# Two decoder layers on one Trainium2 core: the forget-gate strips with the weights as the stationary operand

## Chip, core and metric

The kernel runs on one core of a Trainium2 chip. The metric is device time in microseconds (us) of one execution, the median of several runs. The engines are named as in the profile: PE (TensorE: matmuls), PEld (TensorE's loads of the stationary operand), DVE (VectorE), ACT (ScalarE), POOL (GpSimd), SP (the queue that issues most transfers).

## Reference

Each of two layers computes, for 256 positions of width 2048, a mixer (sliding-window attention beside a gated linear recurrence, HGRN2), a SwiGLU feed-forward part and a gated per-layer embedding. The change touches the forget gate of the recurrence, `hf`, which is 1024 of the 5632 columns of the input projection:

```python
proj = h @ w_in                       # h = rms_norm(x, gain): (256, 2048) @ (2048, 5632)
q, k, v, hq, hf, hi, hg = jnp.split(proj, SPLIT_POINTS, axis=-1)
...
z = hf.astype(jnp.float32)
f = lbf + (1.0 - lbf) * jax.nn.sigmoid(z)
log_f = jnp.log(f)
k_in = (1.0 - lbf) * jax.nn.sigmoid(-z)
hq_ = jax.nn.silu(hq.astype(jnp.float32))
...
o = hgrn2_chunkwise(hq_, k_in, hi, log_f)   # per head of 128 features
```

`rms_norm` divides each position by its own root mean square. The kernel multiplies the gain into the transposed input and applies the factor 1/rms of a position, `rx`, only to the finished product.

## The kernel before

All large products run in "strips" of 512 output columns. A strip takes its weights in chunks of 256 rows. For each chunk `load_w` issues one transfer of 512 KB on SP (tile `wr`), ACT rounds it to an fp32r tile `wh` (line 173) and DVE makes the remainder `wl` (line 174); `wh` and `wl` have 8 buffers each, so that the rounding may run one strip of 8 chunks ahead. The transposed input is kept in the same way as a high and a low part (`xh`, `xl`, both in tiles `ck`), and a product is the sum of three matmuls: xh by wh (line 231), xl by wh (232) and xh by wl (234). In `strip` the input is the stationary operand (128 features by the 128 positions of one half `t`) and the weights are the moving one, 512 columns. The accumulators `acc` then have positions on the partitions and features along the row. One strip of the input projection is 16 row tiles x 2 halves x 3 = 96 matmuls.

After each chunk `tick()` lets other work in: generators that were handed to `start` (attention, recurrence) take one step, and functions that were handed to `later(n, ...)` run n ticks on. That and a scheduler set where the small matmuls stand between those of a strip. Each engine then works through its own list in order.

The strips of the input projection come in this order: keys and values, two strips of attention queries (`done_q(half)`), and then, for each of two groups of four recurrence heads, forget gate, recurrence query, recurrence input, output gate. The recurrence needs its forget gate with features on the partitions. `done_f` (lines 594 to 611) therefore copies the accumulator with the factor `rx` (a scalar for each partition, line 596), and two ticks later `turn` transposes the four blocks on PE (line 601), takes two sigmoids on ACT (603, 604) into `s.f` and `s.k`, and applies the lower bound on DVE (607, 609). This happens for each half `t`, so twice in a strip and 8 times in the program.

The attention on the first query strip runs beside the second one. In it PE computes scores (line 515), DVE takes row maxima, ACT the exponentials (534, 538), DVE the sums (539) and their reciprocals (540). For the second half of the positions, ACT copies scores out of PSUM (526) before DVE masks them (527). Small matmul results stand in four PSUM banks, `ms`, which `bank()` hands out in turn.

Of the kernel before, what the change touches and what calls it, by code (L numbers as in the profile page):

```python
# [8 lines left out]
F32 = mybir.dt.float32  # L9
F32R = mybir.dt.float32r  # L10
I32 = mybir.dt.int32
AF = mybir.ActivationFunctionType
ALU = mybir.AluOpType
AX = mybir.AxisListType

P = 128
SEQ = 256
NT = 2
# [6 lines left out]
W = 512  # L25
# [21 lines left out]
def decoder(ctx: ExitStack, tc: tile.TileContext, x, p, positions, w_in, attn_sinks,  # L47
# [11 lines left out]
    sm = ctx.enter_context(tc.tile_pool(name="sm", bufs=2))  # L59
    pacc = ctx.enter_context(tc.tile_pool(name="pacc", bufs=4, space=PSUM))  # L60
    pms = ctx.enter_context(tc.tile_pool(name="pms", bufs=4, space=PSUM))

    V, S, G, T = nc.vector, nc.scalar, nc.gpsimd, nc.tensor
# [7 lines left out]
    def later(n, fn):  # L71

        queue.append((clock[0] + n, fn))
# [3 lines left out]
    @contextmanager  # L77
    def behind(*names):

        with ExitStack() as st:  # L80
            for n in names:
                st.enter_context(tc.issue_after(marks[n].ins))
            yield
# [3 lines left out]
    def start(gen):  # L87

        running.append(gen)
        if next(gen, True):  # L90
            running.remove(gen)

    def tick():
        clock[0] += 1
        for gen in list(running):
            if next(gen, True):
                running.remove(gen)
        for item in [q for q in queue if q[0] <= clock[0]]:
            queue.remove(item)
            item[1]()  # L100

    def nat(shape=(P, W), dt=F32):
        return np_.tile(list(shape), dt, tag="nat", name="nat")

    def bank(shape=(P, W)):
        return pms.tile(list(shape), F32, tag="ms", name="ms")
# [5 lines left out]
    ident = cp.tile([P, P], F32, name="ident")  # L112
# [11 lines left out]
    ps = bank()  # L124
    T.transpose(ps[:, 0:32], g0rows, ident[0:32, 0:32])
    S.preload_act_table(AF.Copy)
    first = V.tensor_copy(gT[:, 0:32], ps[:, 0:32])
# [39 lines left out]
    def square_sum(src, acc, shape=(P, W)):  # L167
        j = np_.tile([P, W], F32, tag="junk", name="junk", bufs=1)
        S.activation(j[:, 0:shape[1]], src, AF.Square, accum_out=acc)  # L169

    def split(src, hi, lo):

        a = S.copy(hi, src)  # L173
        v = V.tensor_tensor(lo, src, hi.bitcast(F32), op=ALU.subtract)  # L174
        return a, v
# [27 lines left out]
    def new_ck():  # L203
        return [xp.tile([P, 4, SEQ], F32R, tag="ck", name="ck", bufs=14) for i in range(2)]
# [4 lines left out]
    def load_w(w, c, col):  # L209

        raw = wpr.tile([P, 2, W], F32, tag="wr", name="wr")
        nc.sync.dma_start(raw, w[c * 2 * P:(c + 1) * 2 * P, col:col + W].rearrange(
            "(k p) n -> p k n", p=P))
        hi = wps.tile([P, 2, W], F32R, tag="wh", name="wh")
        lo = wps.tile([P, 2, W], F32R, tag="wl", name="wl")
        marks["hi"], marks["lo"] = split(raw, hi, lo)
        return hi, lo

    def strip(lhs, w, col, done, nch=8, row0=0, skew=0, psum=None, pre=None):

        ps = psum or [pacc.tile([P, W], F32, tag="acc", name=f"acc{t}") for t in range(NT)]
        ws = {}

        def part(t, c, lows=(0, 1)):
            hi, lo = ws[c]
            for k in range(2):
                kt = 2 * c + k
                xh, xl = (a[:, kt % 4, t * P:(t + 1) * P] for a in lhs[kt // 4])
                first, last = kt == 0, kt == 2 * nch - 1
                if 0 in lows:  # L230
                    T.matmul(ps[t], xh, hi[:, k], start=first, stop=False)  # L231
                    T.matmul(ps[t], xl, hi[:, k], start=False, stop=False)  # L232
                if 1 in lows:
                    marks[t, c] = T.matmul(ps[t], xh, lo[:, k], start=False, stop=last)  # L234

        for i in range(nch + skew):
            if pre:
                pre(i)
            if i < nch:
                with behind("x") if pre and i == 0 else nullcontext():  # L240
                    ws[i] = load_w(w, row0 // (2 * P) + i, col)
                if pre and i == 0:
                    for t in range(NT):
                        part(t, i, (0,))
                    for t in range(NT):
                        part(t, i, (1,))
                    tick()
                    continue
                part(0, i)
                if i == nch - 1:  # L250
                    done(0, ps[0])
            if i >= skew:
                part(1, i - skew)
            tick()
        done(1, ps[1])

    def load_gain(g, col):
        b = np_.tile([P, W], F32, tag="gB", name="gB", bufs=2)
        nc.sync.dma_start(b, g[col:col + W].partition_broadcast(P))
        return b  # L260
# [22 lines left out]
    def lazy_rstd(ss, name):  # L283
        got = {}

        def get(t):
            if t not in got:
                got[t] = sum_rstd(ss[t], D, f"{name}{t}")
            return got[t]
        return get  # L290


    ones = cp.tile([P, P], F32, name="ones")
# [6 lines left out]
    lb = cp.tile([P, DEPTH, 8], F32, name="lb")  # L300
    omlb = cp.tile([P, DEPTH, 8], F32, name="omlb")
# [101 lines left out]
    xT = [new_ck() for c in range(4)]  # L403
# [21 lines left out]
    for l in range(DEPTH):  # L425

        rx = lazy_rstd(ss, "rx")
        wi = w_in[l]
# [9 lines left out]
        def tables(t):  # L438
            if t not in rot:
                r = rx(t)  # L440
                tb = sm.tile([P, 4, 32], F32, name=f"rot{t}", bufs=1)
                for i, (a, f) in enumerate(((cos, 0.125), (sin, 0.125), (cos, 1.0), (sin, 1.0))):
                    V.tensor_scalar(tb[:, i], a[:, t], r[:, 0:1], f, op0=ALU.mult, op1=ALU.mult)
                rot[t] = tb
            return rot[t]
# [29 lines left out]
        def done_q(half):  # L475
            qT[half] = sp.tile([P, 4, SEQ], F32, tag="AB"[half], name="qT")

            def done(t, ps):
                tb = tables(t)
                o = nat()  # L480
                ov = o.rearrange("p (j g two d) -> p g j two d", j=4, g=2, two=2)
                rotate(ps, tb, 0, 8, ov[:, :, :, 0], ov[:, :, :, 1])
                start(attend(half, t, o))
            return done
# [97 lines left out]
        class Rec:  # L582
# [8 lines left out]
                s.at = sp.tile([P, NT, 4, P], F32, tag="at", name="at")  # L591
                s.ax = sp.tile([P, 4, P], F32, tag="ax", name="ax")

            def done_f(s, t, ps):
                z = nat()
                S.activation(z, ps, AF.Copy, scale=rx(t)[:, 0:1])

                def turn():
                    pt = bank((P, 4, P))
                    for b in range(4):  # L600
                        T.transpose(pt[:, b], z[:, b * P:(b + 1) * P], ident)
                    cols = slice(t * P, (t + 1) * P)
                    S.activation(s.f[:, :, cols], pt, AF.Sigmoid)
                    S.activation(s.k[:, :, cols], pt, AF.Sigmoid, scale=-1.0)
                    for h in range(4):
                        c = s.grp * 4 + h
                        V.tensor_scalar(s.f[:, h, cols], s.f[:, h, cols], omlb[:, l, c:c + 1],
                                        lb[:, l, c:c + 1], op0=ALU.mult, op1=ALU.add)
                        V.tensor_scalar(s.k[:, h, cols], s.k[:, h, cols], omlb[:, l, c:c + 1],
                                        None, op0=ALU.mult)  # L610
                later(2, turn)

            def done_q(s, t, ps):
                sg = nat()
# [176 lines left out]
        if l == 0:  # L791
            with tc.issue_after(first.ins):
                strip(xT, wi, 1024, done_kv, pre=load_x)
        else:
            strip(xT, wi, 1024, done_kv, skew=4)
        for half in range(2):
            strip(xT, wi, half * W, done_q(half))
        for grp in range(2):
            rec = Rec(grp)
            strip(xT, wi, 2560 + grp * W, rec.done_f)  # L800
            strip(xT, wi, 1536 + grp * W, rec.done_q)
            strip(xT, wi, 3584 + grp * W, rec.done_i)
            strip(xT, wi, 4608 + grp * W, rec.done_g)
# [5 lines left out]
        xT = [new_ck() for c in range(4)]  # L809
        mg = []  # L810
        for s in range(4):
            gB = load_gain(post_mix_gain[l], s * W)

            def done(t, ps, s=s, gB=gB):
                if t == 0:
                    mg.append(sp.tile([P, NT, W], F32, tag="ABCD"[s], name=f"mg{s}"))
                V.tensor_tensor(mg[s][:, t], ps, gB, op=ALU.mult)
                square_sum(ps, ssm[t][:, s:s + 1])
                if s == 3:
                    post_norm(mg, ssm, t, ss, xT, gain_cols(32, l, 16), 4)  # L820
# [8 lines left out]
        for gi, glen in enumerate(FF_GROUPS):  # L829
            hid = []  # L830
            for j in range(glen):
                col = (ff0 + j) * W
# [16 lines left out]
            last = gi == len(FF_GROUPS) - 1  # L849
# [22 lines left out]
        xT, ss = nxT, nss  # L872
# [34 lines left out]
        xT, ss = nxT, nss  # L907
# [31 lines left out]
```

## Time and profile before

| | us |
|---|---|
| median of 3 runs | 2488.57 (2486.73 to 2488.8) |
| profiled execution, whole | 2485.5 |
| its span, first to last instruction | 2483.7 |
| PE busy | 2464.8 |
| PEld busy | 2039.7 |
| DVE busy | 1445.0 |
| ACT busy | 1185.1 |

The profiled execution lies 3.1 us under the median of the runs, and 1.8 us of it lie outside the span. Busy times of PE overlap in the sense that a matmul is shown for longer than it keeps the next one waiting; the distance between the starts of two matmuls is the cost of one.

### The profile page before, as it was taken

Reading aid. Unit: us, or ns where it says so; the run is one execution under the profiler, and the core shown is the slowest. Engines: PE = TensorE matmul, PEld = TensorE weight load, DVE = VectorE, ACT = ScalarE, POOL = GpSimd, SP = SyncE. Lnnn points to the kernel's source line nnn. Section 1 sums busy time; section 2 is a strip of 40 time slices with the busy share of each in tenths; the row PEclk is TensorE's granted clock in tenths of the full one; section 3 lists DMA queues with packets and bytes.
Section 4 is the critical chain, followed back from the end, with each engine's and each line's share of the span. In section 5 each row is a group of like instructions: output and inputs, shape, how many; then the busy total and the mean of one; then the engine's idle time right before and its main releaser. Section 6 shows DMA issues by size and latency. Waiting matters only on the chain.

```text
span 2483.7 us, 30796 instructions
## 1 busy us (share of the span) xinstructions
PE 2464.8 (99%) x11597; PEld 2039.7 (82%) x11597; DVE 1445.0 (58%) x1901; ACT 1185.1 (48%) x1684; POOL 98.5 (4%) x213
## 2 busy tenths in 40 slices
PE   8999999999999999999999999999999999999999
PEld 6888887888888888887888888878888888888877
DVE  7786756544554454457567857565445545554574
ACT  6654446444434434446556444464444344444462
POOL 3100001000000000001010000010000000000010
PEclk9999999999999999999999999999999999999999
DMA  7445465666666666664564454656666666666653
GB/s 260 141 144 162 144 197 165 211 190 189 193 189 192 189 193 193 188 201 158 187 203 139 136 172 146 200 176 198 191 191 187 195 189 192 188 193 192 202 171 127
DMA packets 234262, 451.43 MB, mean 182 GB/s; under 512 B 14177, under 2 KB 15105, under 8 KB 234113
## 3 DMA queue, kind: packets, MB, share of 16 engines
q1 hardware_dynamic: 233808, 449.37, 59.1%
q8 instruction: 91, 1.49, 0.2%
q14 instruction: 59, 0.48, 0.1%
q10 hardware_dynamic: 240, 0.07, 0.0%
q0 software_dynamic: 64, 0.02, 0.0%
HBM read 447.31 MB, written 2.10 MB: 181 GB/s over the span
## 4 chain that ended last, share of the span: by engine, by line
PE 95%; DMA 2%; DVE 1%; ACT 1%; issue 0%; POOL 0%; SPq 0%; ACTq 0%; DVEq 0%; POOLq 0%
PE acc L231 29%; PE acc L232 29%; PE acc L234 29%; PE ms L188 2%; DMA wr<-in_w_in_dram 1%; PE ms L676 1%; PE ms L566 1%; DVE wl L174 1%; PE ms L515 0%; ACT wh L173 0%; PE ms L713 0%; ACT junk L169 0%; PE ms L741 0%; PE ms L232 0%; PE ms L234 0%
## 5 line engine op out<-in xcount | busy, mean ns | idle before, releaser
L174 DVE TENSOR_TENSOR wl<-wr,wh 128x1024 fp32r<-128x1024 f32 x840 | 1028.9, 1226 | 942.0 <-ACT wh L173 927.8
L173 ACT CAST wh<-wr 128x1024 fp32r<-128x1024 f32 x840 | 883.7, 1053 | 1121.2 <-PE acc L232 1068.6
L231 PE MATMUL acc<-wh,ck 128*128 128x512 f32 x3328 | 1309.8, 394 | 7.8 <-ACT ck L199 4.7
L232 PE MATMUL acc<-wh,ck 128*128 128x512 f32 x3328 | 1298.4, 390 | 0.9 <-DVE ck L200 0.8
L234 PE MATMUL acc<-wl,ck 128*128 128x512 f32 x3328 | 1297.3, 390 | 0.0
L231 PEld LDWEIGHTS acc<-wh,ck 128*128 128x128 f32 x3328 | 624.9, 188 | 139.5 <-ACT ck L199 10.1
L232 PEld LDWEIGHTS acc<-wh,ck 128*128 128x128 f32 x3328 | 625.6, 188 | 130.3 <-DVE ck L200 4.5
L234 PEld LDWEIGHTS acc<-wl,ck 128*128 128x128 f32 x3328 | 625.1, 188 | 130.8
L199 ACT ACTIVATE ck<-ms,gT 128x128 fp32r<-128x128 f32 x248 | 79.2, 368 | 35.2 <-DVE ck L200 27.7
L200 DVE SCALAR_TENSOR_TENSOR ck<-ms,gT,ck 128x128 fp32r<-128x128 f32 x248 | 75.8, 346 | 19.4 <-ACT ck L199 18.9
L159 POOL TENSOR_TENSOR tiny<-ssf 128x1 f32<-128x1 f32 x4 | 2.1, 535 | 1378.6 <-ACT junk L169 1378.3
L837 ACT ACTIVATE nat<-acc,ry 128x512 f32<-128x512 f32 x44 | 30.2, 687 | 10.7 <-PE acc L234 10.6
L863 DVE TENSOR_TENSOR macc<-acc,macc 128x512 f32<-128x512 f32 x48 | 33.0, 687 | 0.7
L169 ACT ACTIVATE junk<-x 128x512 f32<-128x512 f32 x48 | 30.2, 630 | 6.7 <-DVE x L266 4.1
L843 DVE SCALAR_TENSOR_TENSOR nat<-acc,ry,nat 128x512 f32<-128x512 f32 x44 | 32.4, 748 | 0.1
L174 DVE TENSOR_TENSOR ck<-ms,ck 128x512 fp32r<-128x512 f32 x44 | 30.1, 684 | 0.0
L188 PE MATMUL ms<-ident,x 128*128 128x128 f32 x192 | 27.8, 281 | 1.9 <-DVE x L896 1.2
L188 PEld LDWEIGHTS ms<-ident,x 128*128 128x128 f32 x192 | 22.6, 143 | 8.2 <-DVE x L896 2.4
L188 PEld LDWEIGHTS ms<-ident,nat 128*128 128x128 f32 x184 | 22.8, 139 | 6.4 <-DVE ck L200 0.4
L188 PE MATMUL ms<-ident,nat 128*128 128x128 f32 x184 | 28.0, 272 | 0.0
L459 POOL TENSOR_TENSOR nat<-nat 128x256 f32<-128x256 f32 (+1 forms) x24 | 22.7, 968 | 109.0 <-DVE nat L452 97.6
L534 ACT ACTIVATE nat<-nat,tiny 128x128 f32<-128x128 f32 x64 | 24.8, 390 | 3.9 <-DVE tiny L531 3.6
(198 smaller groups left out, 884.1 us busy)
## 6 DMA issues: line engine op xcount, KB each, us to landing
wr<-in_w_in_dram SPq DMA_DIRECT2D x176, 512.0 KB, 3.8
wr<-in_w_ffn_gate_dram SPq DMA_DIRECT2D x176, 512.0 KB, 3.8
wr<-in_w_ffn_up_dram SPq DMA_DIRECT2D x176, 512.0 KB, 3.7
wr<-in_w_ffn_down_dram SPq DMA_DIRECT2D x176, 512.0 KB, 3.7
wr<-in_w_out_dram SPq DMA_DIRECT2D x64, 512.0 KB, 4.1
wr<-in_w_ple_gate_dram SPq DMA_DIRECT2D x64, 512.0 KB, 4.3
wr<-in_w_ple_proj_dram SPq DMA_DIRECT2D x8, 512.0 KB, 4.2
x<-in_x_dram SPq DMA_DIRECT2D x8, 256.0 KB, 7.6
```

The lines of the kernel that those rows point to most:

```text
L169: S.activation(j[:, 0:shape[1]], src, AF.Square, accum_out=acc)
L173: a = S.copy(hi, src)
L174: v = V.tensor_tensor(lo, src, hi.bitcast(F32), op=ALU.subtract)
L188: T.transpose(ps[:, b], blk, ident)
L199: marks["x"] = S.activation(h[:, b], ps[:, b], AF.Copy, scale=g)
L200: V.scalar_tensor_tensor(lo[:, b], ps[:, b], g, h[:, b].bitcast(F32), op0=ALU.mult, op1=ALU.subtract)
L231: T.matmul(ps[t], xh, hi[:, k], start=first, stop=False)
L232: T.matmul(ps[t], xl, hi[:, k], start=False, stop=False)
L234: marks[t, c] = T.matmul(ps[t], xh, lo[:, k], start=False, stop=last)
L837: S.activation(gate[t], ps, AF.Silu, scale=rx2(t)[:, 0:1])
L843: V.scalar_tensor_tensor(gate[t], ps, rx2(t)[:, 0:1], gate[t], op0=ALU.mult, op1=ALU.mult)
L863: V.tensor_tensor(m, ps, m, op=ALU.add)
```

## The change

The four forget-gate strips are computed by a new function, `strip_T`. In it a block of 128 weight columns is the stationary operand and the input, all 256 positions, is the moving one. The product comes out with features on the partitions, two blocks of 128 features in each accumulator, so that `done_f` needs no transposes. The factor `rx` now runs along the row and no longer along the partitions. A new function `factor_rows`, called once in a layer, lays it out as a tile `rows` (128 x 256, the same in every partition): for each half it multiplies the identity by `rx` on DVE, and PE multiplies a matrix of ones by the result.

```diff
+    def strip_T(lhs, w, col, done, nch=8, row0=0):
+        ps = [pacc.tile([P, W], F32, tag="acc", name=f"acc{i}") for i in range(2)]
+        def part(i, c, hi, lo):
+            for k in range(2):
+                kt = 2 * c + k
+                xh, xl = (a[:, kt % 4] for a in lhs[kt // 4])
+                for b in (2 * i, 2 * i + 1):
+                    o = ps[i][:, (b % 2) * SEQ:(b % 2 + 1) * SEQ]
+                    wb = slice(b * P, (b + 1) * P)
+                    first, last = kt == 0, kt == 2 * nch - 1
+                    T.matmul(o, hi[:, k, wb], xh, start=first and b % 2 == 0, stop=False,
+                             skip_group_check=True)
+                    T.matmul(o, hi[:, k, wb], xl, start=False, stop=False, skip_group_check=True)
+                    T.matmul(o, lo[:, k, wb], xh, start=False, stop=last, skip_group_check=True)
+        for c in range(nch):
+            hi, lo = load_w(w, row0 // (2 * P) + c, col)
+            for i in range(2):
+                part(i, c, hi, lo)
+                if c == nch - 1:
+                    done(i, ps[i])
+            tick()
...
-            def done_f(s, t, ps):
-                z = nat()
-                S.activation(z, ps, AF.Copy, scale=rx(t)[:, 0:1])
-                def turn():
-                    pt = bank((P, 4, P))
-                    for b in range(4):
-                        T.transpose(pt[:, b], z[:, b * P:(b + 1) * P], ident)
-                    cols = slice(t * P, (t + 1) * P)
-                    S.activation(s.f[:, :, cols], pt, AF.Sigmoid)
-                    S.activation(s.k[:, :, cols], pt, AF.Sigmoid, scale=-1.0)
-                    for h in range(4):
...
-                later(2, turn)
+            def done_f(s, i, ps):
+                z = nat((P, 2, SEQ))
+                V.tensor_tensor(z, ps.rearrange("p (h c) -> p h c", h=2),
+                                rows.unsqueeze(1).to_broadcast([P, 2, SEQ]), op=ALU.mult)
+                hh = slice(2 * i, 2 * i + 2)
+                S.activation(s.f[:, hh], z, AF.Sigmoid)
+                S.activation(s.k[:, hh], z, AF.Sigmoid, scale=-1.0)
+                for h in (2 * i, 2 * i + 1):
...
+        rows = sm.tile([P, SEQ], F32, name="rows", bufs=1)
+        def factor_rows():
+            pr = bank((P, NT, P))
+            for t in range(NT):
+                d = nat((P, P))
+                V.tensor_scalar(d, ident, rx(t)[:, 0:1], None, op0=ALU.mult)
+                T.matmul(pr[:, t], ones, d, start=True, stop=True)
+            S.copy(rows, pr.rearrange("p t c -> p (t c)"))
         for half in range(2):
+            if half == 1:
+                later(4, factor_rows)
             strip(xT, wi, half * W, done_q(half))
...
-            strip(xT, wi, 2560 + grp * W, rec.done_f)
+            strip_T(xT, wi, 2560 + grp * W, rec.done_f)
```

Three places show how the lists of the engines change; line numbers of the changed kernel are 26 higher at the attention. The first is PE in layer 1, in the second attention-query strip (`acc_741` and `acc_742` are its accumulators, `acc_742` and `acc_743` in the changed kernel), right behind the scores of the second half. Before:

```order
L515 MATMUL ms<-kT,qT 128x128 x16
L231 MATMUL acc_741<-wh,ck 128x512
L232 MATMUL acc_741<-wh,ck 128x512
L234 MATMUL acc_741<-wl,ck 128x512
L231 MATMUL acc_741<-wh,ck 128x512
L232 MATMUL acc_741<-wh,ck 128x512
L234 MATMUL acc_741<-wl,ck 128x512
```

Now:

```order
L541 MATMUL ms<-kT,qT 128x128 x16
L231 MATMUL acc_742<-wh,ck 128x512
L232 MATMUL acc_742<-wh,ck 128x512
L234 MATMUL acc_742<-wl,ck 128x512
L231 MATMUL acc_742<-wh,ck 128x512
L826 MATMUL ms<-nat,ones 128x128 x2
L232 MATMUL acc_742<-wh,ck 128x512
L234 MATMUL acc_742<-wl,ck 128x512
```

The two matmuls of `factor_rows` (L826) stand four matmuls behind the scores, ahead of the rest of the strip. Layer 2 has them at the same place.

The second place is DVE at the same time, in the softmax of the first half (`tiny` are its row sums). Before:

```order
L539 TENSOR_TENSOR tiny<-tiny 128x4
L540 RECIPROCAL tiny<-tiny 128x4
L539 TENSOR_TENSOR tiny<-tiny 128x4
L540 RECIPROCAL tiny<-tiny 128x4
L527 COPY_PREDICATED nat<-m_prev,ms 128x512 x2
```

Now:

```order
L565 TENSOR_TENSOR tiny<-tiny 128x4
L566 RECIPROCAL tiny<-tiny 128x4
L825 TENSOR_SCALAR nat<-ident,rx_529 128x128
L565 TENSOR_TENSOR tiny<-tiny 128x4
L825 TENSOR_SCALAR nat<-ident,rx_555 128x128
L566 RECIPROCAL tiny<-tiny 128x4
L553 COPY_PREDICATED nat<-m_prev,ms 128x512 x2
```

The operand of the second half (the second L825) now stands behind the second sum (the second L565, L539 before).

The third place is ACT at the end of the first forget-gate strip of layer 1. Before:

```order
L596 ACTIVATE nat<-acc_1041,rx_529 128x512
L173 CAST wh<-wr 128x1024
L554 COPY nat<-ms 128x512
L169 ACTIVATE junk,ssa_150<-ao_148 128x256
L596 ACTIVATE nat<-acc_1042,rx_555 128x512
L173 CAST wh<-wr 128x1024
L603 ACT_TABLE_LOAD
L603 ACTIVATE f<-ms 128x4x128
```

Now:

```order
L626 ACT_TABLE_LOAD
L626 ACTIVATE f<-nat 128x512
L627 ACTIVATE k<-nat 128x512
L626 ACTIVATE f<-nat 128x512
L627 ACTIVATE k<-nat 128x512
L169 ACTIVATE junk,ssa_150<-ao_148 128x256
L580 COPY nat<-ms 128x512
L173 CAST wh<-wr 128x1024
```

The four sigmoids now stand together, ahead of a copy for the attention (L580, L554 before) and of the rounding of the next weights. The number of table loads in the program is the same.

## Rows read from the trace of the kernel before

**Rows 1.** Page, part 1: busy time, share of the span, instructions.
```profile
PE 2464.8 (99%) x11597; PEld 2039.7 (82%) x11597; DVE 1445.0 (58%) x1901; ACT 1185.1 (48%) x1684; POOL 98.5 (4%) x213
```
**Rows 2.** Waits of PE, longest first: us in total, times, longest.
```profile
PE acc L231 <- ACT ck L199: 4.7, 6, 1.4
PE acc L231 <- ACT wh L173: 2.8, 1, 2.8
PE ms L123 <- POOL ident masks.py:199: 1.6, 1, 1.6
```
**Rows 3.** Timeline of PE, forget-gate strip of group 2: start, length, engine, line.
```profile
227.70 0.39 PE L231 MATMUL acc<-wh,ck 128*128 128x512 f32 x1
...
230.88 0.39 PE L234 MATMUL acc<-wl,ck 128*128 128x512 f32 x1
```
**Rows 4.** Timeline of PE near the program's start.
```profile
9.95 0.63 PE L232 MATMUL acc<-wh,ck 128*128 128x512 f32 x1
...
11.65 0.63 PE L232 MATMUL acc<-wh,ck 128*128 128x512 f32 x1
```
**Rows 5.** Windows: busy us and count of each engine, then granted clock.
```profile
3.00:13.50 10.50, 7.69 (x27) 5.97 (x27) 5.84 (x8) 5.48 (x9) 7.62 (x48) 0.84 0.97 343
226.20:238.20 12.00, 12.00 (x55) 9.93 (x54) 5.54 (x6) 6.11 (x7) 0.00 (x0) 1.00 0.68 185
```
**Rows 6.** Chain that ended last: start, us, what, how many in a row.
```profile
128.18 1.73 PE ms L566 x16
...
163.91 2.60 PE ms L713 x16
...
196.54 0.89 PE ms L748 x8
...
239.43 0.44 PE ms L601 x4
```
**Rows 7.** Timeline of PE's weight loads, layer 1.
```profile
121.09 0.19 PEld L231 LDWEIGHTS acc<-wh,ck 128*128 128x128 f32 x1
121.20 0.19 PEld L232 LDWEIGHTS acc<-wh,ck 128*128 128x128 f32 x1
```
**Rows 8.** Instructions of line 123: five matmuls with the same stationary tile.
```profile
L123 PEld LDWEIGHTS ms<-ident x10: 286/333/333, 1.6 to 3.4; 128*128 128x128 f32 x10
```
**Rows 9.** Groups by line: busy, mean ns of one, idle before.
```profile
L601 PE MATMUL ms<-ident,nat 128*128 128x128 f32 x32 | 4.8, 273 | 0.0
L596 ACT ACTIVATE nat<-acc,rx 128x512 f32<-128x512 f32 x8 | 5.5, 684 | 3.1 <-PE acc L234 3.1
L603 ACT ACTIVATE f<-ms 128x512 f32<-128x512 f32 x8 | 4.8, 596 | 1.9 <-PE ms L601 1.9
L609 DVE TENSOR_SCALAR k<-k,omlb 128x128 f32<-128x128 f32 x32 | 8.6, 285 | 0.0
L452 DVE TENSOR_TENSOR nat<-acc,rot 128x512 f32<-128x512 f32 x16 | 10.4, 685 | 2.5 <-POOL nat L459 1.2 <-PE acc L234 0.9 <-issue 0.3
L526 ACT COPY nat<-ms 128x512 f32<-128x512 f32 x8 | 4.2, 573 | 0.0
```
**Rows 10.** Timeline of all engines behind the scores, layer 1.
```profile
79.60 0.39 PE L231 MATMUL acc<-wh,ck 128*128 128x512 f32 x1
...
79.83 0.40 PE L232 MATMUL acc<-wh,ck 128*128 128x512 f32 x1
...
81.26 1.05 ACT L526 COPY nat<-ms 128x512 f32<-128x512 f32 x2
81.38 0.16 DVE L539 TENSOR_TENSOR tiny<-tiny 128x4 f32<-128x4 f32 x1 [1.26 <-ACT tiny L538]
...
81.58 0.18 DVE L540 RECIPROCAL tiny<-tiny 128x4 f32<-128x4 f32 x1
```
**Rows 11.** The same place in layer 2.
```profile
1311.82 0.40 PE L232 MATMUL acc<-wh,ck 128*128 128x512 f32 x1
...
1313.20 1.05 ACT L526 COPY nat<-ms 128x512 f32<-128x512 f32 x2
1313.33 0.16 DVE L539 TENSOR_TENSOR tiny<-tiny 128x4 f32<-128x4 f32 x1 [1.26 <-ACT tiny L538]
```
**Rows 12.** Groups by line, the rounding of the weights on ACT.
```profile
L173 ACT CAST wh<-wr 128x1024 fp32r<-128x1024 f32 x840 | 883.7, 1053 | 1121.2 <-PE acc L232 1068.6
```

More of the change, by code (lines that the diff above doesn't have):

```diff
@@ L592, in __init__ @@
                 s.ax = sp.tile([P, 4, P], F32, tag="ax", name="ax")
-            def done_f(s, t, ps):
-                z = nat()
-                S.activation(z, ps, AF.Copy, scale=rx(t)[:, 0:1])
-                def turn():
-                    pt = bank((P, 4, P))
-                    for b in range(4):
-                        T.transpose(pt[:, b], z[:, b * P:(b + 1) * P], ident)
-                    cols = slice(t * P, (t + 1) * P)
-                    S.activation(s.f[:, :, cols], pt, AF.Sigmoid)
-                    S.activation(s.k[:, :, cols], pt, AF.Sigmoid, scale=-1.0)
-                    for h in range(4):
[L606 to L610, printed above, removed]
-                later(2, turn)
+            def done_f(s, i, ps):
[6 more added lines that the diff above has]
+                for h in (2 * i, 2 * i + 1):
+                    c = s.grp * 4 + h
+                    V.tensor_scalar(s.f[:, h], s.f[:, h], omlb[:, l, c:c + 1],
+                                    lb[:, l, c:c + 1], op0=ALU.mult, op1=ALU.add)
+                    V.tensor_scalar(s.k[:, h], s.k[:, h], omlb[:, l, c:c + 1],
+                                    None, op0=ALU.mult)
             def done_q(s, t, ps):
```

## Prediction

> **What bounds the kernel now.** I read first the busy shares: PE is busy for 99% of the span, DVE for 58%, ACT for 48% [rows 1]. Then the waits: PE's largest are 4.7 us in six pieces and 2.8 us in one [rows 2], so nothing worth naming holds PE up. ACT, on the other hand, sat idle for 1121.2 us ahead of the rounding of weights, 1068.6 of them until PE gave a buffer back [rows 12]. So ACT and DVE run ahead of PE as far as the buffers allow. What counts is therefore how long PE is occupied, and every wait that PE itself gets. Each of the two is added to the time in full, since no slack of PE could take it up.
>
> The cost of a matmul is the distance between starts. In a quiet stretch 15 matmuls of 512 columns start between 227.70 and 230.88, 14 steps of 0.227 us [rows 3], at granted clock 1.00 [rows 5], the 2.4 GHz level. Near the start the distance is 0.425 us (4 steps from 9.95 to 11.65) [rows 4], in a window with a mean granted clock of 0.84 [rows 5]: the 1.2 GHz level. Half of that is 0.213 us. So at full clock 0.213 of the 0.227 us scale with the clock, and some 0.0135 us of each matmul are something else.
>
> **The change part by part.**
>
> *Removed transposes.* 32 transposes in 8 groups of four [rows 9]. A group holds the chain for 0.44 us [rows 6]: 8 x 0.44 = 3.5 us less.
>
> *The strips themselves.* A strip had 96 matmuls of 512 columns and gets 192 of 256: 384 become 768 in four strips, with the same number of columns. Before: 384 x 0.227 = 87.2 us. The trace has no fp32r matmul of 256 columns, so I bound one.
> - From below: a load of a 128-column stationary operand. The products of line 566 have only 64 moving columns and still cost 1.73 / 16 = 0.108 us, those of line 748 with 128 columns 0.89 / 8 = 0.111 us [rows 6]. Two fp32r loads have been 0.11 us apart [rows 7]. A load is issued for every matmul even when the stationary tile stays the same: five products on one tile have ten loads [rows 8] (an f32 product counts as two records). So the repeated `hi` block saves nothing, and 0.110 us is the lower end: 84.5 us, 2.7 less than before.
> - From above: 0.19 us, the whole length of a load [rows 7], if none of it lay beside the matmul before. That is 146 us, 59 more. The 0.11 us between loads speaks strongly against it.
> - Between: 256 columns stream in 0.1065 us. If the 0.0135 us belong to the matmul (its start, or its weight load getting in the way of the stream), one costs 0.120 us, and the strips 92.4 us: 384 x 0.0135 = 5.2 more. If they belong to the columns, one costs 0.1135 us and the strips stay at 87.2.
>
> The f32 products help little: 192 columns cost 2.60 / 16 = 0.1625 us [rows 6], 0.85 ns a column against 0.44 for fp32r, about half the rate, so a share of 0.0135 us could hide there. I take the share as fixed, 0.120 us: a load then runs behind nearly all of every matmul, which is no milder place than now, where it covers half of one.
>
> The Trainium skill's page "TensorE: Matmul & The Clock Gate", section "Back-to-back issue gap", gives N/2.4 + 2.5 ns for a gap at full clock, which is 215.8 ns for 512 columns and 109 ns for 256. The trace disagrees at 512, with 227 ns. By the rule the four strips would take 83.7 us, and the sum below would end 2 us under the time before.
>
> *New wait at `factor_rows`.* The two products stand in PE's list four matmuls behind the scores; in layer 1 that place was reached at 79.83 [rows 10]. Their operands come from DVE, and the second is made behind the second row sum, which started at 81.38 because it waited for exponentials on ACT; the place behind it was free at 81.58 [rows 10]. An operand is a DVE operation on 128 columns, like line 609 with 0.285 us [rows 9]: ready at about 81.87. There is a second reason to wait. The four `ms` banks are handed out in turn, the scores ahead took all four, and the next one is the first of those, which ACT reads with the first of the two copies that started at 81.26 and take 0.573 us each [rows 9, 10]: free at 81.83. Both say that PE can begin the second product at about 81.9, instead of 79.83 for its next matmul: about 2.1 us. The products themselves are four records at 0.111 us: 0.44. Layer 2: from 1311.82 to the copy's end at 1313.77 or the operand at 1313.33 + 0.20 + 0.285 = 1313.82 [rows 11], about 2.0 us, and 0.44. Together 5.0 us more. Nothing else on PE fills the gap, since PE's list is strict, and all that stands behind it is the strip itself. Bounds: 0.9 us, if operands and bank were there in time; 6 us with some latency on each of the steps.
>
> *Evacuation.* For each half of a strip a DVE product from PSUM (like line 452, 0.685 us) takes the place of an ACT copy (0.684), and the sigmoids keep their size (0.596) [rows 9]. DVE's bound operations are half as many and twice as wide. This is less work for ACT and about as much for DVE. It happens earlier, at the end of the strip, and the recurrence query that needs `s.f` is a whole strip later. The waiting instructions hold up what is behind them: on ACT a copy for the attention, whose product on PE comes two ticks later, over 5 us (two chunks of 12 x 0.227), and weight rounding that is a strip ahead. I cost it at nothing. What hides it is the lead of the weight buffers [rows 12]; with that gone it would be 0.685 + 2 x 0.596 + 0.5, some 2.4 us at each of four strips.
>
> *Sum.* -3.5 + 5.2 + 5.0 = +6.7 us. On the profiled execution, 2485.5, that is 2492.2; the median of the runs is 3.1 us higher, and on it I forecast 2495.3.
>
> A difference of 0.2% (5 us) is about what a measurement of this kernel can tell from no change.
>
> **The rivals.**
> 1. *The small share belongs to the columns* (0.1135 us): strips unchanged, -3.5 + 5.0 = +1.5, 2490. This is the case that ends on the other side, no change. For it: at the lower clock the share was not to be seen, as with a limit on how fast fp32r columns are read. Against it: nothing in these rows. It decides from 0.118 us a matmul downwards, where the sum falls under 5 us. Chance 0.30.
> 2. *Matmul and load both at the pace of the loads*, 0.110 us: -3.5 - 2.7 + 5.0 = -1.2, 2487. The f32 rows speak for it, the 0.227 against it. Chance 0.09.
> 3. *Loads and streams hinder each other*, because every stream now has a load beside it for its whole length: at 0.135 us, midway between 0.120 and 0.15, the middle of the two bounds, 103.7 - 87.2 = 16.5 more, 2507. Chance 0.13, falling off above.
> 4. *The wait at `factor_rows` doesn't come*, 4.1 us less: with 0.120 us +2.6, with 0.110 us -5.3 (2483). Chance 0.06, half of it faster.
>
> **How the numbers follow.** My own case has 0.42. Faster by over 0.2% remains only where two favourable sides meet: 0.04. Within 0.2%: rivals 1 and 2, half of 4: 0.42. Slower: my case and rival 3: 0.54. The likeliest time is 2495.3. The range goes from 2487 (rival 2) to 2505, which leaves out the upper half of rival 3 and the faster cases, and holds rival 1. The likeliest case alone: 2493 to 2498.
>
> **What would show it.** The distance between starts of the 256-column matmuls is the main thing: 0.120 us, or 0.1135, or 0.110. PE's waits should have two new ones at line 826, about 2 us each, on ACT's copy or on DVE's operand, in the second query strip of each layer. No line 601 in the chain. No new wait of PE at the end of a forget-gate strip and none for `wh` or `wl`; one there would say that the evacuation isn't hidden. The granted clock should stay at 1.00 through both waits. I am wrong if the distance is below 0.118 us or above 0.125, or if line 826 waits for nothing.

## The result, and the profile after

The changed kernel takes 2493.30 us (median of 8 runs, 2490.64 to 2496.57), the kernel before, beside it, 2486.57 us (8 runs, 2485.39 to 2489.59). The ratio is 1.0024, with the interval 1.0013 to 1.0035: 3 to 9 us slower, 6.7 us by the medians. The profiled execution took 2494.59 us, its span is 2492.7 us, 9.0 more than the span of before.

The page's busy times of the kernel after, as in [rows 1], and its groups by line (count | busy us, mean ns):

```profile
PE 2467.8 (99%) x11957; PEld 2059.2 (83%) x11957; DVE 1445.7 (58%) x1881; ACT 1180.9 (47%) x1678; POOL 98.5 (4%) x213
...
L270 PE MATMUL acc<-ck,wh 128*128 128x256 f32 x256 | 73.9, 289 | 0.0
L273 PE MATMUL acc<-ck,wl 128*128 128x256 f32 x256 | 72.4, 283 | 0.0
L272 PE MATMUL acc<-ck,wh 128*128 128x256 f32 x256 | 72.4, 283 | 0.0
...
L623 DVE TENSOR_TENSOR nat<-acc,rows 128x512 f32<-128x512 f32 x8 | 5.5, 687 | 1.5 <-PE ms L592 1.4
L626 ACT ACTIVATE f<-nat 128x512 f32<-128x512 f32 x8 | 5.0, 624 | 0.0
...
L826 PE MATMUL ms<-nat,ones 128*128 128x128 f32 x8 | 1.4, 300 | 3.7 <-DVE tiny L566 3.7
```

PE has 360 more instructions: 384 more in the strips and 8 more records for the products, 32 transposes fewer. Its busy share hardly moves, and can't tell anything here: a busy PE is at 99% whether a matmul brings 512 columns or 256. What tells is the distance between starts. The timeline of PE in the forget-gate strip of group 2, the place of [rows 3]:

```profile
228.09 0.28 PE L273 MATMUL acc<-ck,wl 128*128 128x256 f32 x1
...
230.97 0.28 PE L273 MATMUL acc<-ck,wl 128*128 128x256 f32 x1
```

These are 24 steps in 2.88 us: 0.120 us each, two of which stand where one of 0.227 stood.

The waits of PE after (in total, times, longest), as in [rows 2]:

```profile
PE acc L231 <- ACT ck L199: 7.6, 8, 1.5
PE ms L826 <- DVE tiny L566: 3.7, 2, 1.9
PE acc L231 <- ACT wh L173: 2.4, 1, 2.4
PE ms L123 <- POOL ident masks.py:199: 1.6, 1, 1.6
```

The second is new. The first is larger than the 4.7 us of [rows 2]; two of its pieces (1.46 and 0.99 us) lie in the program's first 34 us, ahead of the change's first instruction. The answer on line 826's instructions gives both engines that they waited for, PE's loads (ACT) and its matmuls (DVE) apart:

```profile
  ACT nat L552: 4.6, 2
  DVE tiny L566: 3.7, 2
```

The timeline of all engines at that place in layer 1, as in [rows 10]:

```profile
80.88 0.39 PE L231 MATMUL acc<-wh,ck 128*128 128x512 f32 x1
81.31 0.26 DVE L825 TENSOR_SCALAR nat<-ident,rx 128x128 f32<-128x128 f32 x1
...
82.52 1.04 ACT L552 COPY nat<-ms 128x512 f32<-128x512 f32 x2
82.65 0.16 DVE L565 TENSOR_TENSOR tiny<-tiny 128x4 f32<-128x4 f32 x1 [1.09 <-ACT tiny L564]
82.73 0.28 DVE L825 TENSOR_SCALAR nat<-ident,rx 128x128 f32<-128x128 f32 x1
82.93 0.17 DVE L566 RECIPROCAL tiny<-tiny 128x4 f32<-128x4 f32 x1
...
83.14 0.71 PE L826 MATMUL ms<-nat,ones 128*128 128x128 f32 x4 [1.88 <-DVE tiny L566]
...
83.61 0.47 PE L232 MATMUL acc<-wh,ck 128*128 128x512 f32 x1
84.51 0.63 PE L232 MATMUL acc<-wh,ck 128*128 128x512 f32 x1
87.07 0.63 PE L232 MATMUL acc<-wh,ck 128*128 128x512 f32 x1
87.80 0.40 PE L231 MATMUL acc<-wh,ck 128*128 128x512 f32 x1
```

The place is reached at 80.88 + 0.23 = 81.11, and the strip goes on at 83.61: 2.50 us. The second operand (82.73 + 0.28 = 83.01) and the end of ACT's first copy (82.52 + 1.04 / 2 = 83.04) lie 0.1 us before the products. The first product had its operand at 81.31 + 0.26 = 81.57, and yet it starts at 83.14 too: its operand was not what held it. (The profile names line 566, which stands behind the operand's line 825 in DVE's list; the products read what line 825 wrote.) In layer 2 it is the same, and the strip's matmul behind the products starts at 1320.40:

```profile
1317.72 0.39 PE L231 MATMUL acc<-wh,ck 128*128 128x512 f32 x1
...
1319.94 0.71 PE L826 MATMUL ms<-nat,ones 128*128 128x128 f32 x4 [1.83 <-DVE tiny L566]
1320.40 0.47 PE L232 MATMUL acc<-wh,ck 128*128 128x512 f32 x1
```

One difference between the two is in the windows behind them (busy us and count of PE, PEld, DVE, ACT and POOL, then granted clock):

```profile
84.20:87.70 3.50, 3.50 (x10) 2.73 (x9) 2.17 (x5) 1.79 (x4) 0.00 (x0) 0.51 0.11 17
...
1320.40:1323.90 3.50, 3.50 (x18) 2.91 (x17) 3.11 (x6) 2.73 (x6) 0.00 (x0) 1.00 0.02 5
```

Behind the wait in layer 1 the granted clock fell to 0.51 in this window, its 1.2 GHz level. From 84.51 to 87.07 there are 6 steps of 0.427 us in place of 0.227, and with the steps at either end about 1.6 us are lost.

So the 9.0 us between the two spans are made up as follows: strips 768 x 0.120 - 384 x 0.227 = +5.0; the two places at line 826, 2.50 + 2.45 = +4.95; the clock, +1.6; the transposes, -3.5. That is 8.05. The rest isn't the change's: in this execution line 231's matmul ahead of the place in layer 1 starts at 80.88, and at 79.60 in [rows 10], 1.28 us earlier. In two more executions of the changed kernel (a1 and a2 below) it starts at 80.25 and 79.60. From this matmul to the end of the span, where the start of the program no longer counts, the kernel before takes 2483.7 - 79.60 = 2404.1 us and the changed one 2492.7 - 80.88 = 2411.8, which is 7.7 more, of them 1.6 for the clock. In a1, whose clock stayed at 1.00, it is 2490.7 - 80.25 = 2410.4, 6.3 more, beside 5.0 + 4.95 - 3.5 = 6.45 from the terms:

```profile
80.25 0.39 PE L231 MATMUL acc<-wh,ck 128*128 128x512 f32 x1
```

### The profile page after: what moved, and what is told of

Same layout as the page of the kernel before. It is cut to its first block, busy times and chain, and to the rows that moved or that the text cites. A ratio compares the mean times of both kernels' runs of the same rounds, so it can differ in the third digit from the quotient of the medians.

```text
span 2492.7 us, 31494 instructions
## 1 busy us (share of the span) xinstructions
PE 2467.8 (99%) x11957; PEld 2059.2 (83%) x11957; DVE 1445.7 (58%) x1881; ACT 1180.9 (47%) x1678; POOL 98.5 (4%) x213
## 4 chain that ended last, share of the span: by engine, by line
PE 94%; ACT 2%; DVE 2%; DMA 1%; issue 1%; POOL 0%; SPq 0%; ACTq 0%; DVEq 0%; POOLq 0%
PE acc L231 28%; PE acc L232 28%; PE acc L234 28%; PE ms L188 2%; DMA wr<-in_w_in_dram 1%; PE acc L270 1%; PE acc L273 1%; PE acc L272 1%; PE ms L698 1%; PE ms L592 1%; DVE wl L174 1%; ACT wh L173 1%; PE ms L735 0%; ACT junk L169 0%; PE ms L763 0%
## 5 line engine op out<-in xcount | busy, mean ns | idle before, releaser
L231 PE MATMUL acc<-wh,ck 128*128 128x512 f32 x3200 | 1258.3, 394 | 10.1 <-ACT ck L199 7.6
L232 PE MATMUL acc<-wh,ck 128*128 128x512 f32 x3200 | 1249.5, 391 | 0.9 <-DVE ck L200 0.8
L234 PE MATMUL acc<-wl,ck 128*128 128x512 f32 x3200 | 1247.8, 390 | 0.0
L231 PEld LDWEIGHTS acc<-wh,ck 128*128 128x128 f32 x3200 | 601.3, 188 | 137.1 <-ACT ck L199 13.1
L232 PEld LDWEIGHTS acc<-wh,ck 128*128 128x128 f32 x3200 | 601.9, 188 | 125.8 <-DVE ck L200 4.7
L234 PEld LDWEIGHTS acc<-wl,ck 128*128 128x128 f32 x3200 | 601.8, 188 | 125.3
L270 PE MATMUL acc<-ck,wh 128*128 128x256 f32 x256 | 73.9, 289 | 0.0
L273 PE MATMUL acc<-ck,wl 128*128 128x256 f32 x256 | 72.4, 283 | 0.0
L272 PE MATMUL acc<-ck,wh 128*128 128x256 f32 x256 | 72.4, 283 | 0.0
L270 PEld LDWEIGHTS acc<-ck,wh 128*128 128x128 f32 x256 | 49.0, 192 | 0.3
L272 PEld LDWEIGHTS acc<-ck,wh 128*128 128x128 f32 x256 | 49.1, 192 | 0.1
L273 PEld LDWEIGHTS acc<-ck,wl 128*128 128x128 f32 x256 | 49.0, 191 | 0.0
```

Source lines behind the costliest of these rows:

```text
L270: T.matmul(o, hi[:, k, wb], xh, start=first and b % 2 == 0, stop=False, skip_group_check=True)
L272: T.matmul(o, hi[:, k, wb], xl, start=False, stop=False, skip_group_check=True)
L273: T.matmul(o, lo[:, k, wb], xh, start=False, stop=last, skip_group_check=True)
```

## The experiments

The kernel before, run beside the first four, has a median of 2485.79 us (30 runs, 2484.02 to 2489.86).

**The products one strip earlier (e1).** The changed kernel, with one edit:

```diff
-            if half == 1:
+            if half == 0:
                 later(4, factor_rows)
```

> The changed kernel with the two products of the factor row called four ticks into the first attention-query strip, not the second. Theory (three terms: 3.5 us saved transposes, 5.2 us for 768 instead of 384 matmuls, 4.9 us for the wait of PE at the factor row): the wait goes, the products stay, so 4.0 us less than the changed kernel, about +2.6 us on the kernel before (ratio 1.001). If the lower clock behind the wait in layer 1 is its consequence, that stretch goes as well, up to 1.6 us more in executions that have it. Rival (the wait took up slack that PE would have spent elsewhere): no change, ratio 1.0024 on the kernel before.

2486.33 us, ratio 1.0002 (0.9993 to 1.0011): -1.7 to +2.7 us. Line 826 is gone from PE's waits:

```profile
PE acc L231 <- ACT ck L199: 4.7, 7, 1.7
PE acc L231 <- ACT wh L173: 2.9, 1, 2.9
PE ms L123 <- POOL ident masks.py:199: 1.6, 1, 1.6
```

With the wait gone nearly all of the loss is gone. It is 0.5 us by the medians and not the 2.6 that was expected, and PE's timeline in layer 1 shows one reason:

```profile
58.96 0.39 PE L231 MATMUL acc<-wh,ck 128*128 128x512 f32 x1
...
61.91 0.85 PE L826 MATMUL ms<-nat,ones 128*128 128x128 f32 x4
62.59 0.60 PE L497 MATMUL ms<-ident,nat 128*128 128x128 f32 x4
```

In the kernel before PE comes to two of these transposes at 58.96 and waits 1.2 us for POOL; two more stand seven matmuls later:

```profile
60.34 0.44 PE L471 MATMUL ms<-ident,nat 128*128 128x128 f32 x2 [1.22 <-POOL nat L459]
...
62.25 0.39 PE L471 MATMUL ms<-ident,nat 128*128 128x128 f32 x2
```

At 58.96 e1 goes on with the strip instead. All four stand behind the products, the first two 13 matmuls of the strip later than before, and when PE comes to them nothing holds it. So the 1.2 us are gone because the scheduler moved the transposes, and e1 is not the removal of one wait alone. With them, -3.5 + 5.0 + 2 x 0.44 - 1.2 = +1.2 us, inside the interval. Behind this place, from the matmul that starts at 79.60 in the kernel before, e1's span (2484.7) ends 2405.9 us later, 1.8 more than before; -3.5 + 5.0 + 0.44 = 1.9 were to be expected there:

```profile
78.81 0.39 PE L231 MATMUL acc<-wh,ck 128*128 128x512 f32 x1
```

This version ties with the kernel before and doesn't beat it.

**The products alone (e2).** The kernel before, with `rows` and `factor_rows` put in at the place of the change; nothing reads `rows`:

```diff
+        rows = sm.tile([P, SEQ], F32, name="rows", bufs=1)
+        def factor_rows():
...
         for half in range(2):
+            if half == 1:
+                later(4, factor_rows)
             strip(xT, wi, half * W, done_q(half))
```

> The kernel before with only the factor row added, at the place where the changed kernel has it; nothing reads it. Theory: PE waits twice for about 2 us and has 0.45 us of products each time, +4.9 us (ratio 1.0020), and up to 1.6 us more for each wait after which the clock falls. Rival (the wait costs nothing by itself): +0.9 us at most, ratio 1.0004.

2493.38 us (8 runs), ratio 1.0026 (1.0016 to 1.0037): +4 to +9 us. The wait is the one of the change, though no strip is transposed:

```profile
PE acc L231 <- ACT ck L199: 3.9, 7, 1.0
PE ms L804 <- DVE tiny L540: 3.7, 2, 1.9
PE acc L231 <- ACT wh L173: 2.4, 1, 2.4
```

The medians are 7.6 us apart; the 5.0 that were forecast for the products with their wait lie inside the interval. In the profiled execution the clock stayed at 1.00 behind both waits. From the same matmul to the end of its span (2487.8) it takes 2409.3 us, 5.2 more than the kernel before:

```profile
78.54 0.39 PE L231 MATMUL acc<-wh,ck 128*128 128x512 f32 x1
```

That execution is the fastest of the eight (2489.52). Whether a fall of the clock made the others slower, no profile shows.

**The count of matmuls alone (e3).** The kernel before, with the forget strips' matmuls cut into two halves of the weight's columns; x stays the stationary side:

```diff
+                n = W // cut
+                for j in range(cut):
+                    o, wc = ps[t][:, j * n:(j + 1) * n], slice(j * n, (j + 1) * n)
...
-            strip(xT, wi, 2560 + grp * W, rec.done_f)
+            strip(xT, wi, 2560 + grp * W, rec.done_f, cut=2)
```

> The kernel before, where each matmul of the four forget-gate strips is cut into two of 256 weight columns; input still the stationary side, transposes still there. Theory (some 0.0135 us belong to each matmul, whichever operand is stationary): starts 0.120 us apart, +5.2 us, ratio 1.0021. Rival (the extra cost comes from the weights as stationary side, their strided blocks or the block used twice in a row): starts 0.1135 us apart, no change.

2489.74 us, ratio 1.0014 (1.0006 to 1.0023): +1.5 to +5.7 us. PE's timeline:

```profile
227.82 0.28 PE L239 MATMUL acc<-wl,ck 128*128 128x256 f32 x1
...
229.86 0.28 PE L236 MATMUL acc<-wh,ck 128*128 128x256 f32 x1
```

17 steps of 0.120 us, the same as with the weights stationary, and the 5.2 us that were expected lie inside the interval. At these sizes the cost comes with the number of matmuls, not with the side that is held.

**Without the transposes (e4).** The kernel before; the sigmoids read the strip as it is:

```diff
-                    pt = bank((P, 4, P))
-                    for b in range(4):
-                        T.transpose(pt[:, b], z[:, b * P:(b + 1) * P], ident)
+                    pt = z.rearrange("p (b c) -> p b c", b=4)
```

> The kernel before without the 32 transposes of the forget gate: the sigmoids read the copy with positions on the partitions, so the gate enters the recurrence untransposed and that part of the result is left out. Theory: 8 groups of 0.44 us leave PE, -3.5 us, ratio 0.9986. Rival (they stood in gaps of PE): no change.

2483.22 us, ratio 0.9988 (0.9979 to 0.9997): 0.7 to 5.2 us less, which holds the 3.5.

**Cut into four (e5).** Like e3, with `cut=4`; one execution.

> The kernel before, where each matmul of the forget-gate strips is cut into four of 128 weight columns. Theory (0.0135 us belong to each matmul beside its stream, and a weight load of about 0.11 us must fit between two starts): the load bounds, starts 0.11 us apart, 1536 x 0.111 - 87 = +83 us. Rival (the extra adds to the load as well): 0.1245 us, +104 us.

2569.16 us, the kernel before on the same chip 2485.68: +83.5 us. PE's timeline has 20 steps of 0.112 us:

```profile
236.55 0.28 PE L234 MATMUL acc<-wh,ck 128*128 128x128 f32 x1
...
238.79 0.28 PE L239 MATMUL acc<-wl,ck 128*128 128x128 f32 x1
```

Half of the 0.120 us for 256 columns would be 0.060. The distance is that of two loads in [rows 7], 0.11 us; that the load is what sets it is argued, since no run shortens the load at 128 columns.

**What the share of 0.0135 us belongs to (e6, e7, e8, e10).** The operands so far were fp32r, the 4-byte type to which line 173 rounds. Two versions of e1, with 256 columns, and two of the kernel before, with 512. Half of the stationary columns, on e1 and on the kernel before:

```diff
# e6
-                    wb = slice(b * P, (b + 1) * P)
+                    m = P if kt == 0 else P // 2
+                    wb = slice(b * P, b * P + m)
...
# e8
+                m = P // 2 if half and kt else P
+                xh, xl = (a[:, kt % 4, t * P:t * P + m] for a in lhs[kt // 4])
```

The upper 16 bits of every value as bf16, on e1 (e7), and with the same cast for x and the weights on the kernel before (e10):

```diff
+                    wh, wl = (a[:, k, b * P:(b + 1) * P].bitcast(BF)[:, 1::2] for a in (hi, lo))
+                    yh, yl = (a.bitcast(BF)[:, 1::2] for a in (xh, xl))
```

> The changed kernel with the factor row early, and from the second row tile on only 64 of 128 weight columns in each stationary block; the sums of the other 64 features are left out. If the extra 0.0135 us come from the load being in the way of the stream, they shrink with the load: about 0.1135 us between starts, some 5 us less than the factor row early alone. If they belong to the matmul itself: 0.120 us, no change.

> The changed kernel with the factor row early, whose forget-gate strips take only the upper 16 bits of all operands, as bf16; the lower bits are left out of the sums. If the extra 0.0135 us belong to fp32r operands (4 bytes a column): 0.107 to 0.110 us between starts, some 8 us less than the factor row early alone. If every matmul has them: 0.120 us, no change.

> The kernel before; in the forget-gate strips only 64 of the 128 positions of a half are loaded as the stationary side from the second row tile on, with 512 moving columns as ever; the sums of the other positions are left out. If the extra time of a matmul goes with the length of the load beside it (0.0133 us for 128 columns, 0.0067 for 64, whatever the stream): starts 0.220 us apart, not 0.227. If it goes with the columns of the stream: 0.227, no change.

> The kernel before, whose forget-gate strips take only the upper 16 bits of all operands, as bf16, in matmuls of 512 columns as ever; the lower bits are left out of the sums. With 256 columns, halving the bytes of the load (half the stationary columns, or 2 bytes each) halved the extra 0.0133 us; with 512 columns, half the stationary columns did not. If the bytes of all operands set it: starts 0.220 us apart or less. If only short streams show it: 0.227, no change.

PE's timelines, of e6 (16 steps), e7 (17), e8 (21) and e10 (21):

```profile
226.10 0.28 PE L273 MATMUL acc<-ck,wh 128*64 128x256 f32 x1
...
227.91 0.28 PE L274 MATMUL acc<-ck,wl 128*64 128x256 f32 x1
```
```profile
226.06 0.27 PE L272 MATMUL acc<-ck,wh 128*128 128x256 bf16 x1
...
227.99 0.27 PE L275 MATMUL acc<-ck,wl 128*128 128x256 bf16 x1
```
```profile
225.75 0.39 PE L237 MATMUL acc<-wl,ck 128*64 128x512 f32 x1
...
230.57 0.39 PE L237 MATMUL acc<-wl,ck 128*64 128x512 f32 x1
```
```profile
226.10 0.39 PE L235 MATMUL acc<-wh,ck 128*128 128x512 bf16 x1
...
230.83 0.39 PE L235 MATMUL acc<-wh,ck 128*128 128x512 bf16 x1
```

| stationary side | 256 columns | 512 columns |
|---|---|---|
| fp32r, 128 columns | 0.120 | 0.227 |
| fp32r, 64 columns | 0.113 (e6) | 0.230 (e8) |
| bf16, 128 columns | 0.114 (e7) | 0.225 (e10) |

The times follow: e6 2482.29 and e7 2481.55 us, the kernel before on their chip 2485.68; e8 2487.18 beside 2485.77; e10 2485.04 beside 2486.37 (one execution each). Up to e7 it looked as if the share went with the weight load, since a load of fewer columns (e6) halves it at 256 columns, and so do operands of 2 bytes (e7), whose load and stream are both narrower. Only e6's expectation came out: e7 had 0.107 to 0.110 or 0.120, and 0.114 was measured. e8 contradicts the length of the load as the cause: with half a load at 512 columns the distance is neither 0.220 nor 0.227, the two values expected, but 0.230. e10, with the same two values, has 0.225. With bf16 the time goes with the columns (0.1135 x 2 is 0.227, about 0.225), which is what rival 1 said of this kernel; with fp32r and a full load it doesn't.

**The operands one strip earlier (e9).** The changed kernel; DVE makes the operands a strip earlier into tiles of their own, and the products stay in place:

```diff
+        def factors():
+            for t in range(NT):
+                V.tensor_scalar(ds[t], ident, rx(t)[:, 0:1], None, op0=ALU.mult)
...
-                d = nat((P, P))
-                V.tensor_scalar(d, ident, rx(t)[:, 0:1], None, op0=ALU.mult)
-                T.matmul(pr[:, t], ones, d, start=True, stop=True)
+                T.matmul(pr[:, t], ones, ds[t], start=True, stop=True)
```

> The changed kernel, with the two operands of the factor row made one strip earlier into tiles of their own, and the products left where they are. Theory (the wait has two causes that end at about the same time, DVE's operand and the PSUM bank that ACT still reads): PE still waits some 2 us in each layer, now for ACT's copy alone. Rival (the operand alone is the cause): the wait goes, 4 us less.

2494.47 us, beside 2485.77. The wait in layer 1 is as long as before, and now ACT alone ends it:

```profile
82.84 0.71 PE L830 MATMUL ms<-d,ones 128*128 128x128 f32 x4 [1.89 <-ACT nat L552]
```

The bank that ACT's copy still reads is enough for the whole wait: to have the operand early brought nothing, as long as the bank was late. That the operand alone would hold PE as long, with the bank free, is read from its end at 83.01 in the change's timeline; no run shows it.

**The changed kernel twice more (a1, a2).** No edit; for the clock behind the waits.

> The changed kernel once more, for another profile: in how many of its two waits at the factor row the clock falls behind them. If the fall is a chance that each wait takes, some of these profiles show none, some one or two, and each adds about 1.6 us to the span; if the wait of layer 1 always brings it, every profile shows it there.

> The changed kernel a third time, for the same question: whether the clock falls behind none, one or both of the two waits at the factor row, each fall adding about 1.6 us to the span.

2492.66 and 2493.63 us. Windows behind the wait in layer 1, of a1 and of a2:

```profile
83.50:87.00 3.50, 3.50 (x17) 2.84 (x17) 3.10 (x5) 2.74 (x9) 0.00 (x0) 1.00 0.12 16
```
```profile
83.00:85.00 2.00, 2.00 (x6) 1.52 (x6) 1.96 (x4) 0.51 (x2) 0.00 (x0) 0.50 0.00 0
```

With e2 and e9 that makes five profiles with these two waits. In layer 1 the clock fell in three (the one after, a2, e9) and stayed at 1.00 in two (a1, e2); in layer 2 it stayed in all five. What decides it is open.

## Why the prediction was right, point by point

It said 2495.3 us, slower by 6.7; it came to 2493.30, slower by 6.7. That the two differences agree to the digit is luck, with an interval of 3 to 9 us and a cost of the clock that wasn't in the sum; the terms agree on their own, as follows. The 2.0 us between the two figures are the kernel before, whose median beside the changed one was 2486.57 and not 2488.57.

- *Removed transposes, 3.5 us.* Right: line 601 is gone, and e4, which takes nothing else from PE, lies at 2.6 by its medians with 3.5 in its interval.
- *The strips, 0.120 us a matmul, +5.2.* Right in size: 0.120, in the change and in e3, which is +5.0 (768 x 0.120 - 384 x 0.227; the 5.2 is a matter of rounding). The choice between three prices that the rows left open fell on the right one, by the argument that the share is fixed for each matmul; no row decided for it, so some luck is in it. The 0.0135 itself is half of the 0.425 us of the lower clock, taken from 0.227, as if the share weren't paid at the lower clock. A share paid at both clocks would be 2 x 0.227 - 0.425 = 0.029 us, a matmul of 256 columns then 0.128 us and the strips 11 us more; the prediction passes over this case, and the measured 0.120 decides against it. A fixed share holds for fp32r with full loads, at 256 and 512 columns; e6, e7, e8 and e10 show that it isn't a general property of a matmul, and what the share is stays open. Rivals 1 (0.1135) and 2 (0.110) are refuted by the rows, and rival 3 too: a stream with a load beside its whole length pays no larger share (0.120 - 0.1065) than one with a load beside half of it.
- The Trainium skill's page "TensorE: Matmul & The Clock Gate", section "Back-to-back issue gap", gives 109 ns for 256 columns by its formula. The trace disagrees there as it did at 512, with 120 ns, and the gain that would follow from it didn't come; bf16 comes closer, with 114.
- *The new wait, 5.0.* Right: 4.95. e2 shows its price by itself, e1 that nearly all of the loss goes with it, and e9 that the second of the two reasons, the bank, gives the whole wait alone. The first, the operand, ends 0.03 us earlier in the trace and is not shown alone. Rival 4 is refuted.
- *Evacuation at nothing.* Right as far as the rows show: line 623 takes 0.687 us (forecast 0.685), line 626 0.624 (forecast 0.596), nobody on PE waits for either, and `wh` has no new wait.
- *The clock at 1.00 through both waits.* Wrong for layer 1, where it fell in three profiles of five, at 1.6 us in the one shown. This cost wasn't in the sum. It didn't decide the sign: a1, the execution of the change whose profile has 1.00 behind both waits, is slower as well, by 6.9 us (2492.66 beside 2485.77), and by 6.3 from the place in layer 1 to the end.

## What to carry to other kernels

Count a strip's matmuls, not only its columns: 384 more fp32r matmuls at the same columns cost 5 us, about 13 ns each, more than 32 removed transposes gave back. A small product put into the list of an engine that is always busy waits for its operand and for its PSUM bank, and each of them is to be free when the engine gets there; ask of every rotating bank who read it last, and put the product where both come free before the engine does: one strip earlier, in e1, nothing of the wait at the products was left in PE's list of waits. A new place moves other small matmuls too, so read the order of the list again before a gain is put down to the one that was meant.

## What the runs showed of the hardware

- The distance between starts is not one formula of the columns: between 256 and 512 columns it is, with a full fp32r load, 0.013 us and 0.418 ns a column ((0.227 - 0.120) / 256), and with bf16 some 0.002 us and 0.436 ns a column ((0.2252 - 0.1135) / 256). At 128 fp32r columns the first of these would give 0.067 us, and e5 has 0.112. With half of the stationary columns it is shorter at 256 columns (0.113) and longer at 512 (0.230).
- A wait of PE of about 2 us was followed by a stretch at the 1.2 GHz level, at a granted clock of 0.50 to 0.53 over some 3 us, at one place of the program in three profiles of five, and in none of the five at another place with nearly the same wait (1.88 and 1.83 us in the profile of the change).
